# Layer 1's mixer of a two-layer decoder step: the same instructions in another written-down order

## The chip, the cores and the metric

The kernel runs on one core of a Trainium2 chip. The metric is the device time of one execution in microseconds. Before the change it was 1492.82 us (median of three runs, 1492.29 to 1493.84). The core has five engines that the text names: PE (TensorE, the matmuls), DVE (VectorE), ACT (ScalarE), POOL (GpSimd) and SP (SyncE, which here only issues DMAs). Each engine works through its own list of instructions in order; across engines an instruction waits for the data that it reads.

## The reference, cut to what matters

One inference step through two layers, for a prompt of 512 positions and 32 sample positions (8 sequences of 4). Layer 0's mixer is a gated recurrence, layer 1's is a sparse attention: an indexer scores all keys, the best k of them are chosen, and softmax attention runs over those. Both layers also attend to a memory, and end in a gated MLP with a short convolution. The change lies in layer 1's mixer:

```python
def dsa_project(z, pos, q_norm, k_norm, ik_norm):
    q, k, v, iq, ik, iw = jnp.split(z, np.cumsum(DSA_SIZES)[:-1].tolist(), axis=-1)
    q = rope(rms_norm(q...), pos); k = rope(rms_norm(k...), pos)
    iq = rope(iq, pos);            ik = rope(rms_norm(ik, ik_norm), pos)

def indexer_select(iq, iw, ik, q_pos, n_sel):
    dots = einsum('bthd,bsd->bths', iq, ik) * IDX_DIM ** -0.5
    score = einsum('bth,bths->bts', iw * IDX_HEADS ** -0.5, relu(dots))
    vals, idx = lax.top_k(where(allowed, score, -inf), n_sel)

def gathered_attention(q, kg, vg, valid):
    p = softmax(where(valid, einsum('btgrd,btkgd->btgrk', q, kg) * D ** -0.5, -inf))
    return einsum('btgrk,btkgd->btgrd', p, vg)
...
        zp = hp @ w_in_dsa[j]; zs = hs @ w_in_dsa[j]
        tp = dsa_prompt(...); ts = dsa_sample(..., cache_k[j], cache_v[j], page_table)
        mkp, mvp = memory_keys_values(mem_prompt, w_mem_kv[layer], mem_k_norm[layer])
        cp = memory_attention(zp[..., -MEM_WIDTH:], ...); cs = memory_attention(zs[..., -MEM_WIDTH:], ...)
        xp = xp + concatenate([tp, cp], -1) @ w_out[layer]
```

## The kernel before

**Tiles.** Activations are kept with features on the partitions, as eight tiles of 128 x 544 (32 sample columns, then 512 prompt columns). A product in float32 is made as three matmuls on rounded halves: `hi` and `lo` of the activations with `whi` and `wlo` of the weights. The weights come as 199 units of 128 x 1024, numbered from 1 in what follows. A unit is loaded into a tile `raw`, ACT copies it to `whi` (rounded), and `wlo = raw - whi` is made by DVE in one instruction of 128 x 1024 or by POOL in four of 128 x 256 (`Weights._cut`, L791). There are three buffers each of `raw`, `whi` and `wlo`, and a unit is prepared two ahead of its use. In layer 1's mixer POOL's queue also issues the loads of the weights.

**Stages of layer 1's mixer** (from about 744 to 1027 us of the span), with their units: index key (105) and index queries (106 to 109), v (110, 111; products `a_100`, `a_101`), queries 0 to 5 (112 to 117; `a_102` to `a_107`), k (118, 119; `a_108`, `a_109`), memory query (120, 121; `a_110`, `a_111`), memory keys and values (122 to 125; `mkv`), and then the output projection (from 126).

**What runs between them.** Beside these projections some twenty generators do the rest in short steps:
- `index_keys` normalises and rotates the index key (`ikr`) and transposes it on PE (`ikT`); `index_prompt` and `index_sample` make the scores (`isc`, `row_index_sample`).
- `choose_sample` finds the k-th largest score of each sample row by a search with one sum over partitions for each of twelve steps (`tot_1` to `tot_12`) and one at the end. In most of them ACT counts signs against four candidates (`void`) and DVE against three, PE adds the counts over partitions (`tot`), and DVE makes the next candidates with seven small instructions. The trace calls all tiles of this chain `ple_choose_sample` or `e_choose_sample`. `choose_prompt` does the like for three groups of 128 prompt rows with MAX8 and MATCH_REPLACE8 on DVE alone.
- The rotation of a query takes two products on DVE (`rq`, `t2`) and an addition on POOL. `query_scale` makes the queries' norms (`rq` 128 x 30, then `qrb` on PE and `qS`).
- `keys` makes the rotated keys `kr`; SP writes them out (`k_p`). `sample_scores` needs 64 pages of cached keys, that SP loads (`k_sample_scores<-ckT`), and multiplies them in eight parts (`ss_1` to `ss_8`).
- `prompt_attn` (six heads, four groups of rows) takes scores `as`, a softmax (`p`, scaled by `scale_rows`, L917, on ACT or DVE), a transpose `apt` and `ao`. `mem_samples` makes `mb`, `mpt` and `mob` for the sample rows' memory attention.

**What sets the order.** The string SCRIPT (L225), written into the kernel. Wherever a projection asks the pump whether other work is to go in (`run`, `space`, `finish`, `drain`), the characters up to the next `.` are played: each letter is one step of the generator with that index (LETTERS, L224), a number repeats the character behind it. A `+` or `-` answers one choice of engine: for `wlo` + is DVE and - is POOL, for `scale_rows` + is ACT and - is DVE. Every engine then has the instructions in the order in which the program wrote them. All instructions are recorded through one helper, so that the profile shows L420 for each; they are told apart by the names of tiles.

Of the kernel before, what the change touches and what calls it, by code (L numbers as in the profile page):

```python
# [129 lines left out]
def constants():  # L130
# [107 lines left out]
    "uv+w-x3yu/nj2kn/ktux+y2!tz/tut+vwy-zx:ku2;2<2=2>t2k2vz-vwkwu+zk2zkztkv!uwxkv+2x#wuxvw+y!#v2k#+wx-3y4!xky#k#k2#wk"
    "y+xk;<y;=yk!<2!;+-=><+-2;2!<k;=2->!3$<;2-=<=;>-+<2-=;3k<3$;<3k3$<=+-2>=k>k=k2t2u2vt2wt+u2xv2yw2$tu-xy3$uv-w-=>2-"
    "?$t%x-vy-u%&wv%&(xw&()yx()*>y).*,?>*,?.>3.,3?9.+19.+11.+11.+11.+11.+11.+14.-@6.@2.-2.@10.-2.-10.-9.-2.-10.-9.-2."  # L240
    "-10.-9.-2.-10.-9.-2.-10.-9.-2.-10.-9.-2.-10.-9.-2.-10.-9.-2.-10.-9.-2.-10.-9.-2.-8.+8.+8.-8.+8.+8.+8.-8.+8.+8.+"
    "8.-10.-9.-2.-10.-9.-2.-10.-9.-2.-10.-9.-2.-10.-9.-2.-10.-9.-2.-10.-9.-2.-10.-9.-2.-10.-9.-2.-10.-9.-2.-10.-9.-2."
# [2027 lines left out]
```

## Time and profile before

| | us |
|---|---|
| median of three runs | 1492.82 |
| the profiled execution | 1481.36 |
| its span on the core | 1479.6 |
| PE busy in the span | 1428.4 (97%) |
| DVE busy | 797.0 (54%) |
| ACT busy | 587.3 (40%) |
| POOL busy | 578.5 (39%) |

The profiled execution took 11.46 us less than the median of the runs; a change worked out from the trace is carried over to the median as a difference. In the profile's slices of 37 us PE is at 90% or more of nearly all of the span, but for the start and the four slices between about 811 and 959 us.

### The profile page before, as it was taken

To read this page: it belongs to the slowest core of one execution; us is meant where nothing else is said; L and a number is where in the kernel's file an instruction comes from. 1 tells how busy PE (TensorE), PEld (TensorE's weight loads), DVE (VectorE), ACT (ScalarE), POOL (GpSimd) and SP (SyncE) were. 2 spreads that over 40 slices of the span, in tenths; PEclk is the share of its full clock that TensorE was granted. 3 is DMA by queue.
4 is the path that set the end of the run, shared out by engine and by line. 5 is a ranking of instruction groups with operands and counts; after the bars stand their busy time and mean duration, and the time that the engine had idled before them with its cause. 6 is when DMAs were issued, how large, how long until landed. Compare 5 with 4: busy or idle time off the path is not lost.

```text
span 1479.6 us, 28277 instructions
## 1 busy us (share of the span) xinstructions
PE 1428.4 (97%) x11314; PEld 1341.1 (91%) x11314; DVE 797.0 (54%) x1762; ACT 587.3 (40%) x1064; POOL 578.5 (39%) x663
## 2 busy tenths in 40 slices
PE   7989999999999999999999987799999999999998
PEld 7968889999999999999987876466999999999998
DVE  7366877754444224444378879876544442344431
ACT  5447465533333113333326452575333331233320
POOL 4332354423444024446764554460134441144410
PEclk9999999999999999999999997999999999999999
DMA  7341223222322322334322425750223333222331
GB/s 246 129 141 62 75 91 102 89 86 77 99 88 86 100 72 86 91 92 125 123 89 66 152 94 172 238 177 28 86 77 92 93 89 88 82 86 87 92 117 58
DMA packets 58995, 152.54 MB, mean 103 GB/s; under 512 B 7888, under 2 KB 21808, under 8 KB 58864
## 3 DMA queue, kind: packets, MB, share of 16 engines
q1 hardware_dynamic: 49792, 122.84, 27.0%
q0 software_dynamic: 8208, 26.50, 5.4%
q8 instruction: 89, 1.46, 0.4%
q10 hardware_dynamic: 864, 1.40, 0.3%
q14 instruction: 42, 0.34, 0.1%
HBM read 142.23 MB, written 8.47 MB: 102 GB/s over the span
## 4 chain that ended last, share of the span: by engine, by line
PE 84%; DVE 7%; issue 3%; POOL 2%; ACT 2%; DMA 1%; SPq 0%; ACTq 0%; POOLq 0%; DVEq 0%
PE a L420 73%; PE u_hgrn_head L420 1%; POOL wlo L420 1%; PE id_index_prompt L420 1%; PE ho_hgrn_head L420 1%; PE ms_prompt L420 1%; PE hgrn_head_samples L420 1%; PE as_prompt_attn L420 1%; DVE lo L420 1%; PE mkv L420 1%; PE mo_prompt L420 1%; PE sc_hgrn_head L420 1%; DMA raw<-w 1%; PE ao_prompt_attn L420 1%; PE mpt_prompt L420 1%
## 5 line engine op out<-in xcount | busy, mean ns | idle before, releaser
L420 POOL TENSOR_TENSOR wlo<-raw,whi 128x1024 fp32r<-128x1024 f32 (+1 forms) x206 | 353.9, 1729 | 560.1 <-ACT whi L420 536.0
L420 PE MATMUL a<-hi,whi 128*128 128x272 f32 x2640 | 554.6, 291 | 0.8 <-DVE ext L420 0.5
L420 PE MATMUL a<-lo,whi 128*128 128x272 f32 x2640 | 548.9, 289 | 5.6 <-DVE lo L420 5.6
L420 PE MATMUL a<-hi,wlo 128*128 128x272 f32 x2640 | 548.0, 289 | 0.0
L420 PEld LDWEIGHTS a<-hi,whi 128*128 128x128 f32 x2640 | 416.0, 189 | 8.5 <-issue 5.6
L420 PEld LDWEIGHTS a<-lo,whi 128*128 128x128 f32 x2640 | 416.2, 189 | 7.0 <-DVE lo L420 7.0
L420 PEld LDWEIGHTS a<-hi,wlo 128*128 128x128 f32 x2640 | 416.7, 189 | 0.0
L420 ACT ACTIVATE whi<-raw 128x1024 fp32r<-128x1024 f32 (+1 forms) x202 | 209.5, 1038 | 243.9 <-PE a L420 153.6
L420 DVE TENSOR_TENSOR wlo<-raw,whi 128x1024 fp32r<-128x1024 f32 (+1 forms) x59 | 79.4, 1345 | 161.4 <-ACT whi L420 161.2
L420 DVE TENSOR_TENSOR sc<-a,rb 128x544 f32<-128x544 f32 x53 | 38.4, 725 | 114.9 <-PE a L420 113.3
L420 DVE SCALAR_TENSOR_TENSOR conv<-ext,params,conv 128x560 f32<-128x560 f32 x88 | 70.6, 802 | 47.7 <-ACT conv L420 46.2
L420 DVE TENSOR_TENSOR ext<-a,rb 128x240 f32<-128x240 f32 x132 | 37.6, 340 | 105.8 <-PE a L420 98.3
L420 ACT ACTIVATE conv<-ext,params 128x560 f32<-128x560 f32 x44 | 37.7, 856 | 135.0 <-DVE ext L420 114.1
L420 ACT ACTIVATE hi<-sc 128x544 fp32r<-128x544 f32 x44 | 29.0, 659 | 137.5 <-DVE sc L420 137.5
L420 DVE TENSOR_TENSOR x<-a,x 128x544 f32<-128x544 f32 x48 | 34.7, 723 | 78.9 <-PE a L420 78.5
L420 POOL TENSOR_TENSOR sqa<-sqa,sq 128x544 f32<-128x544 f32 x24 | 34.7, 1447 | 107.4 <-ACT sq L420 107.1
L420 DVE TENSOR_TENSOR sc<-sc,conv 128x512 f32<-128x512 f32 x88 | 65.8, 786 | 4.6
L420 ACT ACTIVATE conv<-conv 128x560 f32<-128x560 f32 x44 | 29.6, 672 | 73.8 <-DVE conv L420 73.8
L420 ACT ACTIVATE hi<-x,params 128x544 fp32r<-128x544 f32 x32 | 23.8, 745 | 68.9 <-DVE x L420 68.9
L420 DVE TENSOR_TENSOR lo<-sc,hi 128x544 fp32r<-128x544 f32 x44 | 31.9, 725 | 31.9 <-ACT hi L420 31.9
L420 PE MATMUL a<-whi,hi 128*128 128x256 f32 x160 | 47.0, 294 | 0.0
L420 PE MATMUL a<-whi,lo 128*128 128x256 f32 x160 | 45.1, 282 | 0.0
(406 smaller groups left out, 1918.0 us busy)
## 6 DMA issues: line engine op xcount, KB each, us to landing
raw<-w SPq DMA_DIRECT2D x177, 512.0 KB, 3.5
raw<-w POOLq DMA_DIRECT2D x21, 512.0 KB, 4.1
k_sample_scores<-ckT SPq DMA_DIRECT2D x46, 128.0 KB, 2.1
ck_mem_samples<-cmkT SPq DMA_DIRECT2D x16, 256.0 KB, 5.5
cv_mem_samples<-cmv SPq DMA_DIRECT2D x16, 256.0 KB, 5.6
st_s<-hgrn_head_samples POOLq DMA_DIRECT2D x12, 256.0 KB, 3.0
...
```

The lines of the kernel that those rows point to most:

```text
L420: return f(*args, **kw)
```

## The change

Ten lines of SCRIPT are replaced: of its 3261 symbols those from the 1597th to the 2429th, which is layer 1's mixer. PE and SP issue the same instructions as before in another order. Seven of the splits of weights are made on DVE instead of POOL: units 110 and 111 (v), 112 (query 0), 118 and 119 (k), 126 and 127 (the first of the output projection); each takes four instructions of 128 x 256 off POOL's list and puts one of 128 x 1024 on DVE's. Of `scale_rows`, nine scalings go from DVE to ACT and four from ACT to DVE.

```diff
@@ -231,16 +231,16 @@
...
-    "12.+12.+17.-e6.e2.-2.e8.-5.-2f2.f5.f3.-.f9.-4.f.f9.-gh6.3g.16g2i12gi2gi4gj4gi8gh2g4hjij2h.-ijihjl.lij.i.ji.j.ij."
...
+    "12.+12.+17.-e6.e2.-2.e8.-5.-2f2.f3.f5.+3.f7.+4.f7.f.2g.h.+4.g.g.2g.26gi2g2hi4gigj2i7gighghjig2hjijg.-ghihjilij4."
...
```

The order is moved in all stages. Three places, with the engines' lists before and after:

In the stage of the queries and keys, DVE's list from the rotation of query 3 (`t2_8`) to that of query 4 (`t2_9`). The rows with `choose_sample` make the next candidates of the search from its sixth sum over partitions (`tot_6`), and the last of them is DVE's three counts for `tot_7`. Before:

```order
L420 SCALAR_TENSOR_TENSOR t2_8_9675<-a_105_9573,params1_79,tab_5_9130 64x544 x2
L420 TENSOR_SCALAR ample1_choose_sample1_2_9044<-ample1_choose_sample1_6_9700,ample1_choose_sample1_2_9044 128x7
L420 TENSOR_SCALAR ample1_choose_sample1_1_9043<-ample1_choose_sample1_2_9044 128x1
L420 TENSOR_TENSOR ample1_choose_sample1_1_9043<-ample1_choose_sample1_1_9043 128x7
L420 TENSOR_TENSOR ample1_choose_sample1_1_9043<-ample1_choose_sample1_1_9043 128x1
L420 TENSOR_TENSOR ample1_choose_sample1_1_9043<-consts1_81,ample1_choose_sample1_1_9043 128x7
L420 TENSOR_SCALAR ample1_choose_sample1_1_9048,ample1_choose_sample1_4_9046<-row_index_sample1_3_9039,ample1_choose_sample1_1_9043,ample1_choose_sample1_2_9044 128x264 x3
L420 SCALAR_TENSOR_TENSOR rq_9_9753<-a_106_9687,params1_79,tab_4_9128 128x544
L420 SCALAR_TENSOR_TENSOR t2_9_9754<-a_106_9687,params1_79,tab_5_9130 64x544 x2
```

After:

```order
L420 SCALAR_TENSOR_TENSOR t2_8_9647<-a_105_9564,params1_79,tab_5_9124 64x544 x2
L420 TENSOR_TENSOR wlo_118_9653<-raw_118_9328,whi_118_9652 128x1024
L420 TENSOR_SCALAR ample1_choose_sample1_2_9037<-ample1_choose_sample1_6_9680,ample1_choose_sample1_2_9037 128x7
L420 TENSOR_SCALAR ample1_choose_sample1_1_9036<-ample1_choose_sample1_2_9037 128x1
L420 TENSOR_TENSOR ample1_choose_sample1_1_9036<-ample1_choose_sample1_1_9036 128x7
L420 TENSOR_TENSOR ample1_choose_sample1_1_9036<-ample1_choose_sample1_1_9036 128x1
L420 TENSOR_TENSOR ample1_choose_sample1_1_9036<-consts1_81,ample1_choose_sample1_1_9036 128x7
L420 TENSOR_SCALAR ample1_choose_sample1_1_9041,ample1_choose_sample1_4_9039<-row_index_sample1_3_9031,ample1_choose_sample1_1_9036,ample1_choose_sample1_2_9037 128x264 x3
L420 SCALAR_TENSOR_TENSOR rq_9_9733<-a_106_9656,params1_79,tab_4_9121 128x544
L420 SCALAR_TENSOR_TENSOR t2_9_9734<-a_106_9656,params1_79,tab_5_9124 64x544 x2
L420 TENSOR_TENSOR wlo_119_9742<-raw_119_9458,whi_119_9741 128x1024
```

The `wlo` of the two units of k stand on DVE behind the two rotations, ahead of what follows `tot_6` and `tot_7` in the search.

At the end of k's projection, ACT's list. The row with `choose_sample` is the four counts of signs for the search's eleventh sum, `tot_11`; `sr_1` takes the first part of the sample scores from PE. Before:

```order
L420 ACTIVATE v_10_10063<-a_108_9856,rs_3_8290 128x256 x2
L420 ACTIVATE v_last5_1_10085<-vs_last5_1_10083,rs_3_8290 128x256
L420 ACTIVATE ample1_choose_sample1_1_9047,ample1_choose_sample1_3_9045<-row_index_sample1_3_9039,ample1_choose_sample1_1_9043 128x264 x4
L420 ACTIVATE whi_122_10105<-raw_122_10052 128x1024
L420 ACTIVATE sr_1_9845<-ss_sample_scores1_1_10128 128x256
L420 ACTIVATE ksq_keys1_1_10145<-v_9_10060 128x512
L420 ACTIVATE ksq_keys1_2_10146<-v_10_10063 128x512
```

After:

```order
L420 ACTIVATE v_last5_1_10068<-vs_last5_1_10066,rs_3_8290 128x256
L420 ACTIVATE whi_122_10073<-raw_122_10035 128x1024
L420 ACTIVATE sr_1_9833<-ss_sample_scores1_1_10089 128x256
L420 ACTIVATE ample1_choose_sample1_1_9040,ample1_choose_sample1_3_9038<-row_index_sample1_3_9031,ample1_choose_sample1_1_9036 128x264 x4
L420 ACTIVATE ksq_keys1_1_10188<-v_9_10043 128x512
L420 ACTIVATE ksq_keys1_2_10189<-v_10_10046 128x512
L420 ACTIVATE ksq_keys1_3_10190<-v_last5_1_10068 128x256
```

The split of unit 122 and the taking of `ss_1` now stand ahead of the four counts. On PE `tot_11` now stands right behind `ss_1`, and `ss_1` behind `tot_10`; before, 24 of the 96 matmuls of the memory query's projection stood between `tot_10` and `tot_11`, six of them ahead of `ss_1`.

In the stage of the memory keys, DVE's list from the rotation products of the keys (`t2_keys`, in the trace `t_keys`). `lo_51` is half of the memory's tile that `mkv` reads. Before:

```order
L420 TENSOR_TENSOR t2_keys1_1_10447<-v_9_10060,tt_1_8292 128x2x64 x4
L420 TENSOR_TENSOR t2_keys1_2_10448<-v_10_10063,tt_1_8292 128x2x64 x4
L420 TENSOR_TENSOR t2_keys1_3_10449<-v_last5_1_10085,tt_2_8293 128x2x64 x2
L420 TENSOR_TENSOR lo_51_10492<-mem_5_8769,hi_51_10491 128x512
L420 COPY m_mem_samples2_1_10439<-mst_mem_samples2_2_10504 128x5x2
L420 COPY ample1_choose_sample1_2_9044<-ple1_choose_sample1_13_10544 128x2
L420 SCALAR_TENSOR_TENSOR ample1_choose_sample1_1_9048<-consts0_80,ample1_choose_sample1_2_9044,row_index_sample1_3_9039 128x256
L420 SCALAR_TENSOR_TENSOR ample1_choose_sample1_1_9048<-consts0_80,ample1_choose_sample1_2_9044,row_index_sample1_3_9039 128x8
L420 SCALAR_TENSOR_TENSOR ample1_choose_sample1_1_9048<-ample1_choose_sample1_1_9048,row_index_sample1_3_9039 128x264
L420 SCALAR_TENSOR_TENSOR ample1_choose_sample1_1_9048<-row_index_sample1_3_9039,ample1_choose_sample1_2_9044,ample1_choose_sample1_1_9048 128x264
L420 TENSOR_SCALAR sbias_8304<-ample1_choose_sample1_1_9048 32x256
L420 TENSOR_SCALAR sbias_8304<-ample1_choose_sample1_1_9048 32x8
```

After:

```order
L420 TENSOR_TENSOR t2_keys1_1_10458<-v_9_10043,tt_1_8292 128x2x64 x4
L420 TENSOR_TENSOR t2_keys1_2_10459<-v_10_10046,tt_1_8292 128x2x64 x4
L420 TENSOR_TENSOR t2_keys1_3_10460<-v_last5_1_10068,tt_2_8293 128x2x64 x2
L420 COPY m_mem_samples2_1_10489<-mst_mem_samples2_1_10491 128x5x2
L420 TENSOR_TENSOR kr_2_10062<-kr_2_10062,t2_keys1_1_10458 128x4x64 x2
L420 TENSOR_TENSOR kr_3_10063<-kr_3_10063,t2_keys1_2_10459 128x4x64 x2
L420 TENSOR_TENSOR kr_4_10064<-kr_4_10064,t2_keys1_3_10460 128x2x64 x2
L420 COPY m_mem_samples2_1_10489<-mst_mem_samples2_2_10504 128x5x2
L420 TENSOR_TENSOR lo_51_10513<-mem_5_8767,hi_51_10490 128x512
```

The six additions that end `kr` come ahead of `lo_51`; before they stood behind it and behind the end of the search (`sbias`, eight instructions), from the seventh row behind the rows shown.

Besides: in the index stage 18 matmuls of the last index query's projection are moved ahead of `ikT`, and the `wlo` of units 110 and 111 stand on DVE ahead of `ikr`. In the loop of the search, what follows `tot_2` comes before the rotation of query 0 on DVE and not behind it. The chain of `query_scale` no longer has three instructions of `choose_prompt` ahead of it on DVE, and the end of `mem_samples`' norms comes before `sbias`. The pages of keys on SP stand so that `k_p` comes after 19 pages and not after 21. The heads of `prompt_attn` begin in the order 5, 6, 3, 2, 1, 4 with the `wlo` of units 126 and 127 between them on DVE, and `mpt`, `mob` come later among other work.

## Rows read from the trace of the kernel before

**Rows 1.** The page: busy time of the engines, and the groups of the splits `wlo` on POOL and on DVE (count | busy us, mean ns of one | idle time before them).

```profile
PE 1428.4 (97%) x11314; PEld 1341.1 (91%) x11314; DVE 797.0 (54%) x1762; ACT 587.3 (40%) x1064; POOL 578.5 (39%) x663
...
L420 POOL TENSOR_TENSOR wlo<-raw,whi 128x1024 fp32r<-128x1024 f32 (+1 forms) x206 | 353.9, 1729 | 560.1 <-ACT whi L420 536.0
...
L420 DVE TENSOR_TENSOR wlo<-raw,whi 128x1024 fp32r<-128x1024 f32 (+1 forms) x59 | 79.4, 1345 | 161.4 <-ACT whi L420 161.2
```

**Rows 2.** Busy time by stretches of layer 1's mixer: its length, then busy us of each engine with the count of instructions, the granted clock of PE as a share of full speed, the DMA share and GB/s.

```profile
744.00:811.00 67.00, 63.41 (x466) 52.74 (x464) 50.77 (x117) 29.09 (x66) 37.69 (x75) 0.97 0.19 57
811.00:876.00 65.00, 59.47 (x468) 55.48 (x468) 56.37 (x178) 33.43 (x89) 34.03 (x50) 0.97 0.36 115
876.00:917.00 41.00, 31.97 (x228) 25.99 (x229) 34.36 (x125) 17.64 (x39) 20.10 (x34) 0.79 0.55 172
917.00:954.00 37.00, 28.06 (x191) 18.36 (x193) 31.11 (x112) 18.88 (x56) 12.38 (x20) 0.86 0.75 242
954.00:1027.00 73.00, 67.05 (x516) 42.68 (x512) 58.94 (x178) 51.00 (x148) 32.06 (x33) 0.98 0.38 125
```

**Rows 3.** The timeline of PE: start, length in us, what ran, and in brackets PE's idle time just before and what ended it.

```profile
773.41 0.77 PE L420 MATMUL ikT_index_keys<-consts,ikr 128*64 128x128 f32 x5 [3.41 <-DVE ikr L420]
...
827.75 0.61 PE L420 MATMUL ple_choose_sample<-ple_choose_sample,consts 128*128 128x4 f32 x4 [1.96 <-ACT ple_choose_sample L420]
834.75 0.61 PE L420 MATMUL ple_choose_sample<-ple_choose_sample,consts 128*128 128x4 f32 x4 [0.23 <-ACT ple_choose_sample L420]
...
859.87 0.27 PE L420 MATMUL ple_choose_sample<-ple_choose_sample,consts 128*128 128x4 f32 x1 [1.08 <-ACT ple_choose_sample L420]
...
878.36 0.82 PE L420 MATMUL qrb_query_scale<-consts,rq 32*128 32x32 f32 x6 [2.95 <-DVE rq L420]
...
902.69 1.01 PE L420 MATMUL e_choose_sample<-ple_choose_sample,consts 128*128 128x2 f32 x4 [1.16 <-DVE ple_choose_sample L420]
...
907.52 0.80 PE L420 MATMUL mkv<-whi,lo 128*128 128x512 f32 x1 [3.18 <-DVE lo L420]
...
916.50 0.31 PE L420 MATMUL mb_mem_samples<-consts,rqx_mem_samples 32*128 32x32 f32 x2 [2.10 <-POOL rqx_mem_samples L420]
...
919.79 0.80 PE L420 MATMUL mkv<-whi,lo 128*128 128x512 f32 x1 [1.89 <-DVE lo L420]
...
945.31 0.47 PE L420 MATMUL apt_prompt_attn<-consts,p_prompt_attn 128*128 128x128 f32 x2 [3.47 <-DVE p_prompt_attn L420]
...
953.76 1.25 PE L420 MATMUL ss_sample_scores<-k_sample_scores,qS 128*32 128x256 f32 x15 [1.94 <-ACT ct_prompt_attn L420]
...
959.20 1.93 PE L420 MATMUL mob_mem_samples<-cv_mem_samples,mpt_mem_samples 128*32 128x256 f32 x16 [1.21 <-DVE m_prompt_attn L420]
```

**Rows 4.** Busy time in stretches in which PE's granted clock was at half of full speed: three of the seven, and the sum of all seven (columns as in rows 2).

```profile
829.50:832.90 3.40, 3.40 (x17) 3.40 (x16) 3.25 (x9) 0.70 (x3) 2.19 (x3) 0.50 0.82 274
877.30:884.10 6.80, 5.74 (x34) 4.24 (x34) 4.56 (x26) 4.15 (x13) 2.25 (x5) 0.50 0.78 260
...
959.20:962.60 3.40, 3.40 (x19) 1.42 (x20) 2.26 (x10) 1.36 (x5) 2.49 (x4) 0.51 0.74 239
sum 37.40, PE 30.51 PEld 21.89 DVE 27.66 ACT 11.62 POOL 14.95; mean PE 4.36 PEld 3.13 DVE 3.95 ACT 1.66 POOL 2.14
```

**Rows 5.** The timeline of DVE and POOL in the loop of the search: the addition that ends a query's rotation on POOL, two integer instructions of the search beside it on DVE, and the same two with POOL idle.

```profile
830.72 1.33 POOL L420 TENSOR_TENSOR rq<-rq,t 128x544 f32<-128x544 f32 x1 [2.04 <-DVE t L420]
...
831.11 1.03 DVE L420 TENSOR_TENSOR ple_choose_sample<-ple_choose_sample 128x7 int32<-128x7 int32 x2
...
842.94 0.23 DVE L420 TENSOR_TENSOR ple_choose_sample<-ple_choose_sample 128x7 int32<-128x7 int32 x2
```

**Rows 6.** The timeline of ACT and PE around `tot_11`: the first and the last of the four counts, the split of unit 122, and `tot_11` itself; and a pair of matmuls of a projection at full clock with the next one.

```profile
881.81 0.51 ACT L420 ACTIVATE ple_choose_sample<-row_index_sample,ple_choose_sample 128x264 f32<-128x264 f32 x1 [0.96 <-DVE ple_choose_sample L420]
...
884.24 1.04 ACT L420 ACTIVATE whi<-raw 128x1024 fp32r<-128x1024 f32 x1
...
886.63 0.51 PE L420 MATMUL e_choose_sample<-ple_choose_sample,consts 128*128 128x4 f32 x4
...
769.09 0.41 PE L420 MATMUL a<-hi,whi 128*128 128x272 f32 x2
769.34 0.41 PE L420 MATMUL a<-lo,whi 128*128 128x272 f32 x2
```

**Rows 7.** The timeline of DVE, POOL and SP in the stage of the memory keys.

```profile
902.64 3.82 DVE L420 TENSOR_TENSOR t_keys<-v,tt 128x128 f32<-128x128 f32 x8
...
909.55 1.49 DVE L420 TENSOR_SCALAR sbias<-ple_choose_sample 32x256 bf16<-32x256 f32 x8
911.07 1.83 DVE L420 TENSOR_TENSOR kr<-kr,t_keys 128x256 f32<-128x256 f32 x6
...
916.10 3.63 DVE L420 TENSOR_TENSOR lo<-mem,hi 128x512 fp32r<-128x512 f32 x1
...
916.42 2.77 POOL L420 TENSOR_TENSOR wlo<-raw,whi 128x256 fp32r<-128x256 f32 x4
...
911.86 1.07 SPq L420 DMA_DIRECT2D k_p<-kr  x2
...
924.28 12.92 SPq L420 DMA_DIRECT2D k_sample_scores<-ckT  x12
...
943.47 6.85 SPq L420 DMA_DIRECT2D k_sample_scores<-ckT  x6
```

More of the change, by code (lines that the diff above doesn't have):

```diff
@@ L233 @@
     "-10.-9.-2.-10.-9.-2.-10.-9.-2.-10.-9.-2.-10.-9.-2.-10.-9.-2.-10.-9.-2.-10.-9.-2.-8.+11.+12.+8.+12.+12.+12.+8.+"
-    "12.+12.+17.-e6.e2.-2.e8.-5.-2f2.f5.f3.-.f9.-4.f.f9.-gh6.3g.16g2i12gi2gi4gj4gi8gh2g4hjij2h.-ijihjl.lij.i.ji.j.ij."
-    "ij.ij6.-m2nlilmn.lj.i.ji.ji.ji.j.ij4.-2.n2l2.n3.n4.-2.n2l2.n3.n5.-2lo.o5.lijl.o4.-2.2l10.-.2l15.-q2lp.p7.-lijilp"
-    "q4.j.ijq10.rqrn2l.-z#2s%&()*,tuvwxy!.n.sn2.nlijl2.n.2s.-2l.3n.n4.n6.2/sn3.-/3nlnlns./.n6.-4n3sninj/3t3u3v2w2x2y."
-    "2n6.-ntuwxvy.w.ijnxy.ij.it-3.-u-nv+tw-x-y+/n.uvtj2n.i/nji/juvinw.ji2/2tn2u2vt3wux5.kvy:?wjkjknjt-u-xkt2x:3n/.-nt"
@@ L238 @@
[L238 to L242, printed above, removed]
@@ L243 @@
-    "-8.+8.+8.-8.+8.+8.+8.-8.+24."
+    "12.+12.+17.-e6.e2.-2.e8.-5.-2f2.f3.f5.+3.f7.+4.f7.f.2g.h.+4.g.g.2g.26gi2g2hi4gigj2i7gighghjig2hjijg.-ghihjilij4."
+    "j.ijlj.i.2ji3.g.ji.i.-n3lnm2.jni2.3j2.n.ilnjl2.mi2.-2.i5.n.n2.n.-2.2l3.n7.-2l2.j3.o.2l5.+.o.l.l9.+.lo2.l5.li8.-q"
+    "lp.p7.-ijipql4.l.q.i5.q2.r2.rn.-ltznsnxjl2ju,ly!%w#2.n2.v2slnin.sn2.&sl.-nl.(n)*.n.n2.n4.s3./2./s/n.-2nln.n.sni/"
+    "s4.ln2.-nsn/tntxwuvx.iywu.j2.y.ixy2.+2vujyntwnv2.itwnijuxt+.i2.i.w+.+2nv+ty-j/nwn.tu-2nx-jn.j2/wuvn.ij/u/2tnwujn"
@@ new lines @@
+    "vwxvuxn2.j.t2.ut-ktj:u-kn?nvnt:wkyu/v.-xkukw+v+yxykxyk2nj/x+kwy2tuvty-wu/t+z:;/;uzk<v=>xvz+t<vwu+!>z=x2z!t2kzv!u"
+    "4kwxkwv+x#w+kv2ku>x#!y#+2!yx-xk2yvk!k#!k#;yxy+k<#yk;>;-+#y=<!k!;2!<2-=!;!w<2$;=-+;-+<=;=$<=k;k<+-=2-$k$<$k$k>-+<"
+    "$w<k>k;$>=wtuy$tu>w2t-2xvux3$=wtw+vyu-v$v-uty>-+x-$v?y-%u%&%vw(xw2)xy(?&?*>y=)?>.&,2.>2.*,2?(*,9.+19.+11.+11.+"
+    "11.+11.+11.+14.-@6.@2.-2.@10.-2.-10.-9.-2.-10.-9.-2.-10.-9.-2.-10.-9.-2.-10.-9.-2.-10.-9.-2.-10.-9.-2.-10.-9.-2."
+    "-10.-9.-2.-10.-9.-2.-8.+8.+8.-8.+8.+8.+8.-8.+8.+8.+8.-10.-9.-2.-10.-9.-2.-10.-9.-2.-10.-9.-2.-10.-9.-2.-10.-9.-"
@@ L244 @@
+    "2.-10.-9.-2.-10.-9.-2.-10.-9.-2.-10.-9.-2.-10.-9.-2.-8.+8.+8.-8.+8.+8.+8.-8.+24."
 )
```

## The prediction

> **What bounds the kernel now.** The page comes first: PE is busy for 97% of the span [rows 1], so nothing outside PE's idle time and its clock can give much. The second view is the busy time by stretches, and it says where the idle time is [rows 2]: the index stage lacks 3.6 us of PE work (67.00 less 63.41), the stage of v and the queries 5.5, that of k and the memory query 9.0, that of the memory keys 8.9, the last one 6.0. That is 33.0 us in 283, the whole room of a change that only reorders. The third view is PE's timeline at its waits [rows 3]: PE waits for DVE or for what DVE released (`ikT` 3.41, `qrb` 2.95, the first `mkv` 3.18, the second 1.89, `apt` 3.47), for ACT's counts in the search (1.96, then 0.23 to 1.08), once for POOL (2.10) and at the last part of the sample scores, `ss_8` (1.94). The fourth is the clock. In seven stretches, 37.4 us in all, the granted clock is 0.50, the lower of the two levels (1.2 of 2.4 GHz), and PE was busy in 30.51 us of them [rows 4]; each comes a few us after a wait in rows 3. At the full level that work would take half, so the clock holds another 15.3 us at most.
>
> So three chains set the pace. The search is a loop: two of its sums stand 7.00 us apart on PE (827.75 and 834.75), and PE arrives 0.2 to 1.1 us early in most rounds [rows 3]; what delays a round delays PE. Then DVE: it is busy in 34.36 of 41 us from 876 to 917 [rows 2]. Last SP: from `k_p` on it issues pages at 1.08 to 1.14 us each (12.92 for 12, 6.85 for 6) until 950.3 [rows 7], and `ss_8` begins 3.4 us later [rows 3].
>
> **The change part by part.** I sum at two points, the start of `ss_8` and the end of the mixer, since what is won ahead of `ss_8` counts only as far as `ss_8` itself comes earlier.
>
> *Index stage.* 18 matmuls now fill part of the wait for `ikT`. Two matmuls take 0.25 us at full clock (769.09 to 769.34, [rows 6]), so they cover 9 x 0.25 = 2.25 of 3.41 us. Against that, two splits of 1.35 us each [rows 1] stand on DVE ahead of `ikr`: 2.7 later if DVE has no slack there, and the wait is then 3.41 + 2.70 - 2.25 = 3.86. Bounds -2.25 and +0.45. POOL no longer makes these two splits beside DVE's small instructions, so some of the 2.7 comes back; I take the middle, -1.0.
>
> *The loop.* What follows `tot_2` is no longer behind a query's rotation, so the 1.96 wait should go, and with it perhaps the half clock from 829.5, where 3.40 us of work would take 1.70. Bounds -3.7 and -1.9. But `wlo` of units 118 and 119 now stand on DVE ahead of what follows `tot_6` and `tot_7` (1.35 each, 2.7). The cover there is thin: PE waits in most rounds already. They may cost more. POOL's addition of 1.33 us falls on the same place, and the two integer instructions beside it take 1.03 us, against 0.23 with POOL idle [rows 5]. If split and addition go one after another, a round loses 1.35 + 1.33 less the 0.80 that it loses now, 1.88, and two rounds 3.8. Taken: -3.7 for the first place (the wait is short, and the clock fell only behind waits), +2.7 for the second, together -1.0, with bounds -3.7 (both splits hidden) and +1.9 (3.8 less 1.9).
>
> The Trainium skill, "SBUF — State Buffer", section "SBUF: two separate sides", states that DVE and POOL share a pair of ports as an exclusive lock that the first holds for its whole instruction. The trace agrees that DVE is held, by the 1.03 us against 0.23, and by the `lo` of 3.63 us that ran beside POOL's four splits of 2.77 us; the latter shows DVE held over several instructions of POOL, not one. By that rule the loop's term is the +1.9; by the plain length of the instructions it is the -1.0 that I use.
>
> *Around `tot_11`.* The 2.95 us wait for `qrb` should go, since three instructions of `choose_prompt` leave DVE's path to it. In its place PE gets a wait: after `tot_10` only the eight matmuls of `ss_1` stand ahead of `tot_11`, and ACT does the split of unit 122 (1.04 us) and takes `ss_1` before its four counts. The four counts took 2.4 us (881.81 to 884.24). So PE would stand for about 3 us, with bounds 1.5 and 6.5 (if the load of unit 122 is late), and the 24 matmuls that covered it before (3.0 us at 0.125) come later. `tot_11` itself comes at most a little earlier than 886.63 [rows 6]. I cost it at nothing. The work that hides it is the wait of PE at the end of the search and the first `mkv`, 1.16 + 3.18 us [rows 3]: what PE does later here it does there instead of standing. If DVE were ready early there, it would cost the 3.0.
>
> *Keys and memory keys.* On DVE the end of `kr` comes ahead of `lo_51`, which costs the first `mkv` 1.83 us [rows 7]; if POOL's split no longer runs beside the `t_keys` (3.82 us for eight of the ten), as much may come back. So 0 to +1.8 for the first `mkv`. The norms of `mem_samples` no longer stand behind `sbias` (1.49) and the end of the search, so the 2.10 wait for POOL goes, and the second `mkv`, held by a `lo` of 3.63 us, starts 0 to 2.7 earlier. `kr` ends 4.2 us earlier (912.9 less 1.83 behind 906.9, [rows 7]). SP has 19 pages ahead of `k_p` and not 21, so two more come behind it, 2 x 1.14: its last page is issued 1.9 earlier.
>
> *Attention.* The heads start in another order, and two splits (2.7 us) go into DVE's row between the softmaxes. The wait of 3.47 for `apt` partly goes, since fillers leave its place. These two about cancel; bounds -3.5 and +2.7.
>
> *Behind `ss_8`.* `mpt` and `mob` stand behind other work: the wait of 1.21 [rows 3] should go, and the half clock from 959.2 (3.40 us, worth 1.70, [rows 4]) may. Bounds -2.9 and 0; I take -1.5, the middle.
>
> The scalings that change engine are under 0.4 us each, off the path but in the attention, and inside its bounds.
>
> *The sum.* By its pages `ss_8` comes 1.0 + 1.0 + 1.9 = 3.9 earlier, but the attention's splits stand on the other way to it, 2.7 of them; `ss_8` waits for the later. I take -1.0 for `ss_8` and -1.5 behind it: **-2.5 us**. On the profiled execution's 1481.36 that is 1478.9; the median of the runs lies 11.46 us above that execution, and I carry the difference over: 1492.82 - 2.5 = 1490.3.
>
> **The rivals.** *B, all pieces hold.* The loop is 3.7 earlier (POOL's load falls and the splits hide), `ss_8` comes with its pages by some 4.7 us, and behind it 2.9 with the half clock: -7.6, 1485.2. For it: every one of the larger waits in rows 3 has its releaser moved up, and each wait that goes takes a stretch of half clock along. Against it: DVE gets 7 x 1.35 = 9.4 us more, in stretches in which it is the engine waited for.
>
> *C, the loop pays (slower).* The splits of units 118 and 119 go one after another with POOL's additions: +1.9 at k's end; `kr` ahead of `lo_51` adds 1.8 to the first `mkv`, and the splits between the softmaxes 2.7; less the 1.5 behind: +4.9, 1497.7. It decides once PE's waits ahead of `tot_8` and `tot_9` sum to over 4 us and the first `mkv` begins after 909. For it: PE waits for the search in most rounds, and DVE for POOL in rows 5. Against it: 4.3 us of idle time at `mkv` take up what comes late.
>
> *D, another wait takes the place of each.* The sums of rows 2 stay and only the places differ: 0, 1492.8. For it: the 3 us at `tot_11` against the 2.95 at `qrb` are just that.
>
> **How the numbers follow.** Forecast 0.42 (own range -5.0 to 0), B 0.22, C 0.20, D 0.16. A measurement can tell about 0.2%, 3.0 us, from no change. Faster by more than that: B, and 0.18 of the forecast's 0.42, together 0.40. Within it: 0.24 of the forecast, and 0.15 of D: 0.39. Slower: C and 0.01 of D: 0.21. The range reaches to B and 1.4 us beyond, for part of the attention's bound of -3.5, and to C: 1483.8 to 1497.7, which leaves out a tenth on each side.
>
> **What would show it.** In the profile after: PE's wait of 1.96 at `tot_3` gone; waits ahead of `tot_7` to `tot_9` of 1 to 2.5 us; a wait of about 3 at `tot_11`, none over 1 at `qrb` and none for POOL at `mb`; the last page of keys issued near 947 to 949; PE busy between 811 and 954 us in some 2 us more than the 119.5 of rows 2. Wrong would be: the integer instructions beside `wlo` on DVE at over 2 us, first `mkv` after 909 (then C), or a granted clock near 1.0 from 876 to 954 (then B).

## The result and the profile after

| | median us (range, runs) |
|---|---|
| before | 1492.55 (1490.95 to 1496.36, 6) |
| after | 1515.49 (1510.44 to 1520.74, 6) |

The ratio is 1.0138, 95% interval 1.0115 to 1.0161: slower by 22.9 us. The profiled execution of after took 1510.44 us, its span 1508.7. The same kernel before takes about 1481 us beside f1 to f4, as in the profile of before, and about 1495 beside the other experiments, as in the runs compared here; the g runs bear on why.

The page of after, busy time of the engines, which answers to the first line of [rows 1]:

```profile
PE 1434.8 (95%) x11314; PEld 1342.0 (89%) x11314; DVE 795.7 (53%) x1764; ACT 591.6 (39%) x1069; POOL 562.0 (37%) x635
```

The work is the same, but PE lacks more of its span, and is busy 6.4 us longer, so more of it ran at the lower clock. Two stretches of after, from k's first matmul (`a_108`) to `ss_8` and from there to the first matmul of the output projection (`a_112`), columns as in [rows 2]:

```profile
860.40:957.20 96.80, 76.75 (x549) 58.59 (x548) 79.70 (x286) 43.41 (x110) 36.00 (x60) 0.87 0.56 178
957.20:1057.30 100.10, 79.35 (x516) 48.91 (x516) 54.64 (x174) 54.85 (x154) 30.36 (x32) 0.83 0.28 90
```

Before, the same two took 93.4 and 73.4 us (from 860.34 to 953.76 to 1027.13). So k's projection begins at the same time in both profiles, `ss_8` 3.5 us later, and the last stretch takes 26.7 us more. That k begins at the same time is chance: after had begun the index key's projection 1.7 us earlier, ahead of which nothing is changed, and took 1.7 us longer from there to k. PE's timeline of after at its waits, which answers to [rows 3]:

```profile
813.56 0.61 PE L420 MATMUL ple_choose_sample<-ple_choose_sample,consts 128*128 128x2 f32 x4 [1.74 <-ACT ple_choose_sample L420]
...
839.40 0.80 PE L420 MATMUL ple_choose_sample<-ple_choose_sample,consts 128*128 128x4 f32 x3 [5.09 <-ACT ple_choose_sample L420]
...
878.55 0.50 PE L420 MATMUL qrb_query_scale<-consts,rq 32*128 32x32 f32 x6 [1.57 <-DVE rq L420]
...
885.38 1.02 PE L420 MATMUL e_choose_sample<-ple_choose_sample,consts 128*128 128x4 f32 x4 [4.23 <-ACT ple_choose_sample L420]
...
910.77 0.80 PE L420 MATMUL mkv<-whi,lo 128*128 128x512 f32 x1 [2.68 <-DVE lo L420]
...
957.21 2.24 PE L420 MATMUL ss_sample_scores<-k_sample_scores,qS 128*32 128x256 f32 x16 [4.62 <-ACT ct_prompt_attn L420]
...
963.38 1.61 PE L420 MATMUL as_prompt_attn<-kT,rq 128*128 128x384 f32 x2 [2.98 <-issue]
...
969.07 0.69 PE L420 MATMUL apt_prompt_attn<-consts,p_prompt_attn 128*128 128x128 f32 x2 [4.08 <-ACT sr L420]
```

Three long waits are new: at `tot_5` (839.40), at `tot_11` (885.38) and at `ss_8` (957.21). Behind `ss_8` PE stands for ACT and DVE, and these two stand for something that the profile doesn't name. ACT and DVE of after there ("remote": a releaser that is not seen):

```profile
963.12 0.20 ACT L420 ACTIVATE sr<-sn_sample_scores 128x32 f32<-128x32 f32 x1 [3.26 <-remote]
...
968.82 0.20 ACT L420 ACTIVATE sr<-sn_sample_scores 128x32 f32<-128x32 f32 x1 [5.49 <-remote]
...
968.90 0.56 DVE L420 CUSTOM_DVE_ANT_0 p_prompt_attn<-as_prompt_attn,isc_index_prompt 128x384 f32<-128x384 f32 x1 [8.89 <-remote]
```

Both wait for sums of PE that by PE's timeline are long made: `sn` begins at 958.92 and takes 0.96 us, ACT takes its second half at 968.82; `as` begins at 963.38 and takes 1.61, DVE has it at 968.90. The profile of before has no such wait.

### The profile page after: what moved, and what is told of

It reads as the page before. It is cut to its first block, busy times and chain, and to the rows that moved or that the text cites. A ratio compares the mean times of both kernels' runs of the same rounds, so it can differ in the third digit from the quotient of the medians.

```text
span 1508.7 us, 28253 instructions
## 1 busy us (share of the span) xinstructions
PE 1434.8 (95%) x11314; PEld 1342.0 (89%) x11314; DVE 795.7 (53%) x1764; ACT 591.6 (39%) x1069; POOL 562.0 (37%) x635
## 5 line engine op out<-in xcount | busy, mean ns | idle before, releaser
L420 POOL TENSOR_TENSOR wlo<-raw,whi 128x1024 fp32r<-128x1024 f32 (+1 forms) x178 | 334.5, 1888 | 561.3 <-ACT whi L420 542.8
L420 DVE TENSOR_TENSOR wlo<-raw,whi 128x1024 fp32r<-128x1024 f32 (+1 forms) x66 | 88.1, 1335 | 166.4 <-ACT whi L420 160.3
```

The lines of the kernel that those rows point to most:

```text
L420: return f(*args, **kw)
```

## The experiments

**Halves of the order.** e1 to e4 join the two orders at points where both have played the same steps. e1 has the changed order up to the search's end (ahead of `tot_11`'s step) and then the order before; e2 the reverse; e3 the changed order for the last stretch alone (from about `ss_8`); e4 all of it but that. The line with the join, e1 and e4 against the changed kernel, e2 and e3 against before:

```diff
e1
-    "lp.p7.-ijipql4.l.q.i5.q2.r2.rn.-ltznsnxjl2ju,ly!%w#2.n2.v2slnin.sn2.&sl.-nl.(n)*.n.n2.n4.s3./2./s/n.-2nln.n.sni/"
+    "lp.p7.-lijilpq4.j.ijq10.rqrn2l.-z#2s%&()*,tuvwxy!.n.sn2.nlijl2.n.2s.-2l.3n.n4.n6.2/sn3.-/3nlnlns./.n6.-4n3sninj/"
...
e3
-    "uv+w-x3yu/nj2kn/ktux+y2!tz/tut+vwy-zx:ku2;2<2=2>t2k2vz-vwkwu+zk2zkztkv!uwxkv+2x#wuxvw+y!#v2k#+wx-3y4!xky#k#k2#wk"
+    "2ukw+v+2ykxyk2nj/x+kwy2tuvty-wu/t+z:;/;uzk<v=>xvz+t<vwu+!>z=x2z!t2kzv!u4kwxkwv+x#w+kv2ku>x#!y#+2!yx-xk2yvk!k#!k#"
...
```

e2 and e4 have the other side of the same joins.

> The changed order up to the end of the queries' projections (index stage and the loop of the search, with the splits of units 110, 111, 112, 118 and 119 on DVE), the order of before from there on. In the two profiles the changed kernel is 0.04 us behind at the first matmul of k's projection. Theory 1 (the loss lies behind ss_8, in the last stretch of the mixer): within 4 us of before. Theory 2 (the loss is begun early and grows: what comes late in the loop delays all that follows): slower by over 8 us.

> The order of before up to the end of the queries' projections, the changed order from there on (k's projection, memory keys, attention, the last stretch). Theory 1: slower by 17 to 30 us, about as the changed kernel. Theory 2: slower by under 12 us.

> The order of before up to the end of the memory's projection, the changed order in the last stretch alone (from about ss_8 to the output projection; three steps that the changed order has earlier are put at its head). Theory 1: slower by 15 to 27 us. Theory 3 (the last stretch is late since heads of attention, loads and the POOL queue arrive there in another state): slower by under 6 us.

> The changed order up to the end of the memory's projection, the order of before in the last stretch (three steps that before has earlier are put at its head). Theory 1: slower by 2 to 7 us, what ss_8 is late by. Theory 3: slower by 15 us or more.

Against before (1495.85): e1 1499.69, ratio 1.0024 (1.0007 to 1.0042); e2 1514.28, 1.0108 (1.0073 to 1.0143); e3 1500.33, 1.0024 (1.0006 to 1.0041); e4 1503.27, 1.0041 (1.0016 to 1.0065). So the larger part lies behind the search, and the last stretch costs more behind the changed middle: by the ratios e2 costs 16 us and e3 3.6. Theory 2 falls, since e1 costs little and e2 much. Theory 1 fits e1 and e4 but not e3, for which it had 15 to 27 us, and theory 3 fits e3 but not e4, for which it had 15 or more (6 by the ratio): neither the last stretch alone nor all ahead of it alone makes the loss. In e1 too ACT and DVE have waits without a seen releaser, of 4.45 and 4.61 us, in the order before; the profile of before has none, so f1 to f4 took that up.

**Is the profile of before typical?** f1 is the kernel before once more; f2 has the changed order between the two joins only; f3 is the changed kernel with the seven splits back on POOL, f4 the kernel before with the same seven on DVE. f3's edit in the first two of its three lines (f4's is the like):

```diff
-    "12.+12.+17.-e6.e2.-2.e8.-5.-2f2.f3.f5.+3.f7.+4.f7.f.2g.h.+4.g.g.2g.26gi2g2hi4gigj2i7gighghjig2hjijg.-ghihjilij4."
-    "j.ijlj.i.2ji3.g.ji.i.-n3lnm2.jni2.3j2.n.ilnjl2.mi2.-2.i5.n.n2.n.-2.2l3.n7.-2l2.j3.o.2l5.+.o.l.l9.+.lo2.l5.li8.-q"
+    "12.+12.+17.-e6.e2.-2.e8.-5.-2f2.f3.f5.-3.f7.-4.f7.f.2g.h.-4.g.g.2g.26gi2g2hi4gigj2i7gighghjig2hjijg.-ghihjilij4."
+    "j.ijlj.i.2ji3.g.ji.i.-n3lnm2.jni2.3j2.n.ilnjl2.mi2.-2.i5.n.n2.n.-2.2l3.n7.-2l2.j3.o.2l5.-.o.l.l9.-.lo2.l5.li8.-q"
```

> The kernel before, unchanged, profiled once more. The profile that the prediction rests on shows 1481.36 us, 11 us under the median of the runs. Theory A (that execution was an unusual one; others have stops of several us behind ss_8, in which PE's finished matmuls are reported late and DVE and ACT stand): 1489 to 1499 us, the last stretch from ss_8 to the first matmul of the output projection 82 to 88 us instead of 73.4. Theory B (the profile was typical, and the stops belong to the changed order): 1480 to 1484 us and 73 to 75 us.

> The changed order only from the end of the queries' projections to the end of the memory's projection (k's projection, tot_9 to tot_13, memory keys, first steps of the attention); the order of before ahead of it and behind it. Changed middle and changed last stretch together were slower by 1.08%, the last stretch alone by 0.24%. Theory 4 (the two belong together: the changed last stretch is dear only when it is entered in the changed state): slower by 0 to 5 us. Theory 6 (the middle is the dear part by itself): slower by 9 us or more.

> The changed order with the seven splits (units 110, 111, 112, 118, 119, 126, 127) back on POOL in four pieces each; nothing else differs from the changed kernel. Theory 5 (the splits on DVE are what is paid for): 8 us or more faster than the changed kernel, so under 1% slower than before. Theory 4: within 4 us of the changed kernel, so 1.1 to 1.6% slower than before.

> The order of before with those seven splits on DVE in one piece each; nothing else differs from before. Theory 5: slower by 8 us or more. Theory 4: within 4 us of before.

f1 took 1481.27 us, with 76.1 in the last stretch, which fits theory B but for 1.1 us there. Against before (1481.31 here): f2 1484.74, 1.0020 (1.0005 to 1.0034); f3 1488.71, 1.0042 (1.0030 to 1.0054); f4 1484.48, 1.0021 (1.0007 to 1.0035). None of these profiles has a wait of 1 us or more without a seen releaser there. Even so the middle costs 3 us, the splits on DVE 3, and the changed order without those splits 6 (7.4 by the medians). Theory 4 fits f2 and f4 and not f3, theory 5 fits f3 and not f4; the changed kernel itself was not timed beside these, so they don't show what its loss is without such waits.

**The stops and the gathers.** These waits without a seen releaser are called stops from here on. They stand where POOL issues 32 indirect gathers of index keys (about 690) and 32 of cached values (957 to 1025). g1 is the changed kernel again. g2 (changed) and g3 (before) make all 64 with plain DMAs of the same tiles from fixed rows, and so leave out the reading by index; g4 is e3 again.

```diff
-        G.indirect_dma_start(out=out, out_offset=None, in_=src,
-                             in_offset=bass.IndirectOffsetOnAxis(ap=idx, axis=0))
+        k = fixed[0] % (src.shape[0] // 128)
+        fixed[0] += 1
+        G.dma_start(out=out, in_=src[128 * k:128 * k + 128, :])
```

> The changed kernel unchanged, timed beside the three below on one chip. Theory 'order and stops': the new order costs some 8 to 10 us by itself (the last stretch +4 to +6 through TensorE's half clock, the seven splits and the middle some 1 to 3 each) and the rest of the measured 23 us comes on top only on a chip whose executions show the stops of some 3 to 9 us whose releaser is not seen ('remote'). If the kernel before takes about 1481 us here and no stops show, the ratio is 1.005 to 1.008; if it takes about 1495 us and stops show, 1.011 to 1.016. Rival 'order alone': the ratio is 1.012 to 1.016 on any chip, with or without the stops.

> The changed kernel with the 64 indirect gathers that GpSimd issues (32 of index-key rows, 32 of cache-value rows) replaced by plain DMAs of the same tiles and sizes on the same queue, from fixed rows: which cache rows are read is no longer the one that the page table says. Theory 'stops belong to the gathers': the waits released by nothing that is seen go away at 680 to 740 and at 955 to 1025 us, and the time stands 1.005 to 1.008 above the kernel before with the same replacement (the run beside this one), whatever chip it is. Rival 'stops come from elsewhere' (the chip's other traffic, the profile): the stops of 3 to 9 us stay at the same places, and the distance stays that of the run with gathers. On a chip without stops both say 1.005 to 1.008, and the run then only prices the gathers.

> The kernel before with the same 64 indirect gathers replaced by plain DMAs from fixed rows (so which cache rows are read is changed). Theory 'stops belong to the gathers': on a chip with stops this falls by 8 to 15 us below the kernel before, to some 1481 to 1486 us; on a chip without, it stays within 3 us of it. Rival 'stops come from elsewhere': within 3 us on either chip.

> The order before up to the step ahead of the first scores against the sample's keys (ss_8), and the changed order for the whole last stretch behind it, as in e3_tail, now beside the changed kernel on the same chip. Theory 'order and stops': the last stretch costs +4 to +6 us without stops (ratio 1.003 to 1.004), the larger part of what the whole change costs there, and PE's clock falls to half for some 10 us behind 968; with stops 1.002 to 1.008. Rival 'the last stretch is dear only in the state in which the changed order enters it': within 1 us (1.000 to 1.001) without stops.

Against before (1494.81): g1 1512.97, 1.0122 (1.0090 to 1.0155); g2 1491.31, 0.9978 (0.9961 to 0.9996); g3 1477.37, 0.9888 (0.9863 to 0.9913); g4 1499.96, 1.0030 (1.0007 to 1.0053). No wait without a seen releaser is left in g2 or g3, and before falls by 17.4 us (8 to 15 were expected), the changed kernel by 21.7. So the stops belong to the gathers, but not to them alone: with the same gathers f1 to f4 have none. What else they need stays open. The chip's number doesn't decide it: on record it is 13 for the f runs and for the g runs. The eight profiles with stops (after, e1 to e4, g1, g4, i1) hold some 700 semaphore records less than the twelve without (10,288 to 10,378 against 11,036 to 11,054), so that a share of the profile's recording isn't excluded. Without the stops 13.9 us remain (1491.31 less 1477.37), more than the 8 to 10 expected: most of the loss is the change's own. It can now be placed, since the two plain kernels differ by the change alone. (With the stops the changed last stretch takes 91.4 us in g4 and 94.3 in e3, behind the order before, and 99 to 103 behind the changed middle, in e2, after and g1; the order before takes 85.2 to 85.9 there in e1, e4 and i1. Without them the same two read 79.1 and 80.3, in h2 and g2 below. So what the middle and the last stretch cost on top of each other came with the stops.) The stretches of g3 and then of g2, cut as above:

```profile
858.80:951.10 92.30, 74.39 (x548) 56.36 (x548) 78.16 (x284) 42.49 (x110) 39.95 (x68) 0.87 0.58 184
951.10:1023.10 72.00, 65.95 (x517) 42.33 (x517) 58.97 (x178) 51.22 (x149) 19.40 (x33) 1.00 0.37 129
```

```profile
865.30:960.30 95.00, 74.83 (x549) 57.15 (x548) 79.10 (x286) 43.30 (x110) 36.96 (x61) 0.89 0.59 181
960.30:1040.60 80.30, 72.19 (x517) 46.77 (x517) 54.08 (x174) 54.57 (x154) 17.16 (x33) 0.90 0.35 112
```

In the last stretch PE stands 8.1 us against 6.05, and is busy 6.2 us longer for the same matmuls: the granted clock is 0.90 against 1.00, and this is most of the 8.3.

**The pieces, without stops.** All with the plain DMAs: h1 is g2 with the edit of f3, h2 has the join of e3, h4 that of f2. h3 is g2 with one step moved, the chain on `m_rest` (the norms of the memory's second keys, letter `:`):

```diff
-    "vwxvuxn2.j.t2.ut-ktj:u-kn?nvnt:wkyu/v.-xkukw+v+yxykxyk2nj/x+kwy2tuvty-wu/t+z:;/;uzk<v=>xvz+t<vwu+!>z=x2z!t2kzv!u"
+    "vwxvuxn2.j.t2.ut-ktju-kn?nvntwkyu/v.-xkukw+v+2:yxykxyk2nj/x+kwy2tuvty-wu/t+z:;/;uzk<v=>xvz+t<vwu+!>z=x2z!t2kzv!u"
```

> The changed kernel with plain DMAs from fixed rows in place of the 64 indirect gathers, and the seven splits of units 111, 112, 114, 118, 119, 122 and 123 back on GpSimd. Beside 1491.3 us with them on VectorE. Theory 'holds': what the splits cost is where VectorE's small operations of the search come to stand beside four split operations in a row of GpSimd (a 128x7 pair took 3.88 us at 837 where it took 1.03 before, and TensorE waited 5.09 us behind it), and moving the splits shifts those meetings: 1484 to 1489 us, the waits at tot_5 and tot_11 below 3 us. Rival 'work': the splits only move some 1.3 us each between engines that have time: within 2 us of 1491.3.

> With the same plain DMAs: the order before up to ss_8, the changed order behind it. Theory 'the last stretch costs by itself': from ss_8 to the first matmul of the output projection 78 to 81 us (before 72.0, the changed kernel 80.3 in the profiles with plain DMAs), with a stretch of half clock of about 12 us behind some 966, and 1483 to 1486 us in all against 1477.4. Rival 'only in the changed state': 72 to 74 us and 1477 to 1479.

> The changed kernel with plain DMAs, and one step, the inverse norms of the memory's second keys (the 14 operations on m_rest and two on kr, VectorE, 5 us in the profile), put behind the two reciprocals for which ScalarE and then ss_8 wait. Theory 'a long chain of VectorE ahead of what is waited for': the wait of 4.75 us at ss_8 falls to 0.5 to 2 us, the stretch of half clock behind it is shorter, and the time falls by 2 to 5 us below 1491.3. Rival 'the wait only moves' (the steps behind come later by the same 5 us): the wait at ss_8 goes and the waits behind it grow by as much, within 1.5 us.

> With the same plain DMAs: the changed order only from the end of the sample's search (tot_11) to ss_8, the order before ahead of it and behind it. Theory 'three parts add up': the changed kernel's 13.9 us are some 7 for the last stretch, some 5 for this one (waits at tot_11, the first piece of the memory's keys 3 us later, ss_8's 4.75 us) and the rest for the loop with its splits, so 1480 to 1484 us. Rival 'the middle is paid only where the loop is changed': 1477 to 1479.

(The seven units are those that the section on the change names; h1's expectation has other numbers.) Against before (1497.03): h1 1486.84, 0.9936 (0.9914 to 0.9957); h2 1484.40, 0.9919 (0.9891 to 0.9947); h3 1491.01, 0.9969 (0.9949 to 0.9989); h4 1485.72, 0.9929 (0.9907 to 0.9951). By stretches, from the starts of six matmuls in each profile (index key's projection, query 3's, k's, `tot_12`, `ss_8`, output projection), us:

| | to query 3 | to k | to `tot_12` | to `ss_8` | to output | ratio |
|---|---|---|---|---|---|---|
| g3, before | 95.4 | 25.9 | 28.6 | 63.7 | 72.0 | 0.9888 |
| g2, changed | 93.6 | 31.4 | 32.6 | 62.4 | 80.3 | 0.9978 |
| h1, splits on POOL | 91.7 | 26.0 | 33.2 | 62.3 | 80.3 | 0.9936 |
| h2, last stretch | 95.9 | 25.1 | 28.6 | 62.3 | 79.1 | 0.9919 |
| h3, step moved | 93.6 | 31.5 | 32.6 | 59.8 | 80.3 | 0.9969 |
| h4, middle | 96.5 | 25.1 | 32.8 | 64.9 | 72.4 | 0.9929 |
| i2, loop, splits on POOL | 91.7 | 29.8 | 28.2 | 63.7 | 72.0 | 0.9899 |

g2 less g3 is -1.8, +5.6, +4.0, -1.3 and +8.3, with -1.1 behind that: 13.6 by the profiles, near the medians' 13.9. (The two profiled executions differ by 16.4; the other 2.7 lie ahead of the index key, where nothing is changed.) In the profiles each piece costs where it stands, and alone about as much as with the others: the last stretch 7.2 in h2, the way to `tot_12` 4.2 in h4. The times bear this out less closely, since the h runs were not timed beside g3: h2 costs 4.6 us by the ratios and 7.0 by the medians, h4 6.1 and 8.4. h2's theory holds, its rival falls; h4's rival falls, and its time is 1.7 us above what its theory gave, though inside it by the ratio. h1 fits 'holds' in time and at `tot_5` (1.99 us), not at `tot_11`, where PE still waits 5.86. Two slices of h2's last stretch, at half clock (972.00 to 980.00):

```profile
972.00:976.00 4.00, 4.00 (x28) 1.56 (x27) 2.07 (x4) 2.17 (x6) 0.00 (x0) 0.50 0.00 0
976.00:980.00 4.00, 3.53 (x19) 2.35 (x12) 1.64 (x6) 2.19 (x4) 0.00 (x0) 0.50 0.00 0
```

and the waits of PE ahead of it:

```profile
963.03 0.71 PE L420 MATMUL spt_sample_attn<-consts,sr 128*128 128x128 f32 x4 [1.01 <-ACT sr L420]
...
969.40 0.55 PE L420 MATMUL apt_prompt_attn<-consts,p_prompt_attn 128*128 128x128 f32 x3 [1.41 <-DVE m_prompt_attn L420]
```

The first waits for ACT, which now also scales `sr` (1.18 us, where DVE did it in 0.77 before); the second for DVE, which has three MAX8 and MATCH_REPLACE8 pairs of `choose_prompt` ahead of a head's softmax. That these two bring the half clock is read from the order of the rows and not tried.

h3's step did what it was moved for: PE of g2 at `ss_8`, then of h3 there and behind it,

```profile
960.32 2.24 PE L420 MATMUL ss_sample_scores<-k_sample_scores,qS 128*32 128x256 f32 x16 [4.75 <-ACT ct_prompt_attn L420]
```

```profile
955.72 0.82 PE L420 MATMUL ss_sample_scores<-k_sample_scores,qS 128*32 128x256 f32 x6 [0.97 <-ACT ct_prompt_attn L420]
...
960.35 0.33 PE L420 MATMUL sn_sample_scores<-ktn,qS 128*32 128x32 f32 x16 [2.54 <-DVE m_prompt_attn L420]
...
961.54 0.44 PE L420 MATMUL sn_sample_scores<-ktn,qS 128*32 128x32 f32 x16 [0.86 <-ACT sr L420]
```

The wait of 4.75 us at `ss_8` is 0.97, and 2.54 and 0.86 stand behind it, at `sn`. The profile keeps 2.6 us of it (59.8 against 62.4, with 80.3 behind in both). The time is that of g2 within the interval, 0.3 us less by the medians and 1.3 by the ratios: the rival, that the wait only moves, is nearer by the time, though 1 to 3 us can't be told.

**Is the loop a gain?** From the index key to k, h1 takes 117.7 us and g3 121.2. i1 has e1's order with its five splits on POOL, i2 the same with plain DMAs. i1's edit to e1 is the diff of f3 above, its two lines.

> The changed order through the index and the search's loop up to tot_11, with its five splits there back on GpSimd, and the order before from there to the end; gathers as in the kernel before. Theory 'the loop is better by 3 to 4 us once the splits don't hold VectorE' (from a_95 to a_108 117.7 us with the splits on GpSimd, 121.2 in the order before, both with plain DMAs): 3 to 4 us below the kernel before, 0.9970 to 0.9985. Rival 'entered earlier, the rest waits longer' (what is gained ahead of tot_11 is given back at the first piece of the memory's keys): 0.9990 to 1.0010.

> The same order with plain DMAs from fixed rows in place of the 64 indirect gathers. Theory 'the loop is better': 1473 to 1475 us, against 1477.4 for the order before with plain DMAs (in another call); from a_95 to a_108 117 to 118.5 us, and from a_108 to the first matmul of the output projection 163 to 166 us as before (164.3). Rival 'given back': from a_108 167 to 169 us, and 1476 to 1479 in all.

Against before (1495.02): i1 1494.70, 1.0001 (0.9983 to 1.0018); i2 1480.62, 0.9899 (0.9873 to 0.9924). No gain. The theory falls, and not by the rival's place: the 3.7 us won up to query 3 are given back before k (29.8 against 25.9), with the order and the engines of h1, which takes 26.0 there. So the splits' engine isn't the larger part of what is lost there. DVE's pair of integer instructions ahead of `tot_5`, and POOL beside it, in i2 and then in h1:

```profile
830.38 3.94 DVE L420 TENSOR_TENSOR ple_choose_sample<-ple_choose_sample 128x7 int32<-128x7 int32 x2
...
830.13 1.37 POOL L420 TENSOR_TENSOR rq<-rq,t 128x544 f32<-128x544 f32 x1
831.45 2.76 POOL L420 TENSOR_TENSOR wlo<-raw,whi 128x256 fp32r<-128x256 f32 x4
```

```profile
834.25 1.05 DVE L420 TENSOR_TENSOR ple_choose_sample<-ple_choose_sample 128x7 int32<-128x7 int32 x2
...
833.86 1.35 POOL L420 TENSOR_TENSOR rq<-rq,t 128x544 f32<-128x544 f32 x1
835.18 2.79 POOL L420 TENSOR_TENSOR wlo<-raw,whi 128x256 fp32r<-128x256 f32 x4
```

In i2 the pair begins 0.25 us behind POOL's addition and ends when the four splits have ended; in h1 0.39 behind, and it ends with the addition. With POOL idle it takes 0.23 [rows 5]; what it takes longer beside POOL is called a hold below. All profiles divide so. Where POOL's addition waits for DVE's products the pair begins 0.39 to 0.40 behind it and takes 1.03 to 1.06 us (twelve profiles, each that has the order before in the loop, and f3 and h1). Where POOL is late with the splits ahead, and starts when it comes free, the pair begins 0.24 to 0.30 behind and takes 3.88 to 3.94 (after, g1, g2, h3, e1, e4, i1, i2: eight of eight), and PE waits 5.09 to 5.15 at `tot_5`.

The way from the index key to k can so be taken apart, by single profiles: the order wins 3.5 us (117.7 in h1 against 121.2 in g3), the hold costs 3.8 (121.5 in i2 against 117.7), and the five splits on DVE cost another 3.5 in g2 (125.0 against 121.5). With the gathers the splits cost less: after and g1 take 1.0 us longer than i1 there, e1 1.7.

No version beats the kernel before: i1 equals it, and g3 reads fixed rows.

## Why the prediction was wrong

Forecast were -2.5 us, range -9.0 to +4.9; measured +22.9. The direction was rival C's, and two of the marks named for it came: the integer pair took 3.88 us, and the first `mkv` began at 910.77, after 909. The third, waits of over 4 us ahead of `tot_8` and `tot_9`, did not: PE waited 1.64 there, and the long wait stood at `tot_5`. Of the forecast's own signs the wait at `tot_3` went, but one of 1.74 came at `tot_2`; `qrb` kept 1.57; the pages of keys were issued until 952.7 us, not 949; and PE was busy for 116.5 us between 811 and 954, 3 less than before and not 2 more.

- **Index stage, -1.0: right.** PE's wait of 3.41 at `ikT` became 1.34 and 0.94.
- **The loop, -1.0 with bounds -3.7 and +1.9: the hold was priced too low.** With the index stage, forecast at -2.0 together, the way to k took 1.7 us more in after than in before, and 3.8 more in g2 than in g3. The gain was there: without the hold, from the index key to k, f3 takes 118.2 and h1 117.7 us, against 121.6 in f2 and 121.2 in g3. But the price of POOL's work beside the search was put at the 1.03 us of [rows 5], and the `lo` of 3.63 in [rows 7], held for four splits, stood in the same text as a case by itself. The pair took 3.88, and PE stood 5.09. The splits on DVE, costed at 2.7 for two of them, cost 1.0 to 3.5 for all five.
- **Around `tot_11`, costed at nothing: the cover failed.** The wait was 4.23 us in after, 5.4 to 5.9 in the kernels with the changed middle and no stops, inside the bounds of 1.5 to 6.5; the load of unit 122 was late, as the upper bound had it. ACT of after:

```profile
881.59 1.06 ACT L420 ACTIVATE whi<-raw 128x1024 fp32r<-128x1024 f32 x1 [1.40 <-DMA raw<-w]
882.55 0.37 ACT L420 ACTIVATE sr<-ss_sample_scores 128x256 f32<-128x256 f32 x1
882.82 0.50 ACT L420 ACTIVATE ple_choose_sample<-row_index_sample,ple_choose_sample 128x264 f32<-128x264 f32 x1
```

  What failed is the cover. `tot_12` came 4.0 us later (32.6 against 28.6), and the 4.3 us of idle time at the search's end and at `mkv` didn't take it up: there PE waits for the end of a row on DVE that has no slack. Between the search step that takes `tot_11` and `lo`, DVE has no idle time of 0.15 us in any profile. From `tot_11` to `lo` it is 19.9 to 20.2 us in the ten profiles with the order before there and 23.4 to 24.7 in the ten with the changed one, since the additions of `kr` come into the row (1.8 to 3.3 us) and DVE is held in it for longer; in after 3.68 us by POOL's products of the keys, at an instruction that took 0.25 before. DVE of before, then DVE and POOL of after:

```profile
902.39 0.25 DVE L420 TENSOR_TENSOR ple_choose_sample<-ple_choose_sample 128x1 f32<-128x1 f32 x1
```

```profile
900.21 3.68 DVE L420 TENSOR_TENSOR ple_choose_sample<-ple_choose_sample 128x1 f32<-128x1 f32 x1
903.81 2.49 DVE L420 TENSOR_TENSOR t_keys<-v,tt 128x128 f32<-128x128 f32 x8
...
900.09 3.37 POOL L420 TENSOR_TENSOR kr<-v,tt 128x128 f32<-128x128 f32 x8
```

- **Keys, 0 to +1.8 for the first `mkv`: +3.25** (910.77 against 907.52), at the end of that row, which was 4.5 us longer in after while `tot_11` came 1.25 earlier; the text moved `t_keys` out of POOL's way and didn't ask what came in.
- **`ss_8`, -1.0: +3.5 in after.** Of that most was there at `mkv`; the attention then kept it. `ss_8` waited for a head's `ct` on ACT, and that for two reciprocals of DVE behind the `m_rest` chain; the pages on SP, by which the term was made, were not what came last. The rule that the later of two decides was right, but a third was later.
- **Behind `ss_8`, -1.5 with bounds -2.9 and 0: +7.2 alone, +8.3 in the whole.** The largest error. The term counted one wait that goes (1.21) and its half clock, and nothing that the new order might put there; a stretch in which 517 matmuls stand in a new order had a bound of 0 above it. Most of the cost is clock: of g2's 8.3 us 6.2 are matmuls at the lower level, 2.1 waits.
- **The carry-over to the median.** The profile had no stops, and the runs of the median, by their time, had them (1481.36 against 1492.82); so the forecast took the change for the same with and without stops. The order before takes 85.2 to 85.9 us from `ss_8` to the output projection with stops (e1, e4, i1) and 72.0 without; the changed order 100.1 and 103.2 (after, g1) and 80.3. So the stops cost it some 20 to 23 us there and the order before 13 to 14. By the medians of the g runs: 18.2 us with the gathers (1512.97 less 1494.81), 13.9 without, 4.2 by the stops.

So the steps that failed are the price of a hold, the cover at `tot_11`, the bound of 0 behind `ss_8` and the carry-over, in that order of time; by size the stretch behind `ss_8` is the first. In sum: 13.9 us belong to the change by itself, and 4 to 9 to what the stops add to it; 22.9 in the first comparison and 18.2 in the second have intervals that overlap. D was wrong as well: waits didn't change places one for one.
